# Ten groups of an MLP's up projection by one Strassen step, in a fused encoder layer on one core

## The chip, the cores and the metric

One core of a Trainium2 chip runs the whole layer in one launch. The metric is device microseconds of that launch. Five engines have their own instruction queues and run side by side, held in step by semaphores: TensorE (PE; the loading of its stationary operand is listed apart, as PEld), VectorE (DVE), ScalarE (ACT), GpSimd (POOL) and SyncE (SP), which issues most DMAs.

## The reference

One layer of a streaming encoder on x of 512 tokens by 1024 features, in float32: three mixers and their output projection, cross-attention into 256 memory tokens, and a gated MLP. The change touches the MLP alone, whose weights are 1024 x 5632 (up) and 2816 x 1024 (down); the residual that goes into it is called h2 in the kernel:

```python
def conv_ffn(xn, w_up, conv_w, conv_b, w_down):
    h = xn @ w_up
    a, b = jnp.split(h, 2, axis=-1)
    rhs = conv_w.reshape(CONV_W, 1, D_FF).astype(a.dtype)
    c = lax.conv_general_dilated(a, rhs, window_strides=(1,), padding=[(CONV_W - 1, 0)],
                                 dimension_numbers=('NWC', 'WIO', 'NWC'),
                                 feature_group_count=D_FF) + conv_b
    return (jax.nn.gelu(c, approximate=False) * b) @ w_down
...
        h = h + conv_ffn(rmsnorm(h, ffn_norm_g[l]), ffn_w_up[l], ffn_conv_w[l],
...
```

## The kernel before

All activations lie transposed, features on the 128 partitions and the 512 tokens along the free axis, so a matrix product is a sum over tiles of 128 features. Full float32 accuracy comes from `mm3` (lines 344 to 346): each operand is held as an exact high and low part of 12 bits each, and a product is three matmuls, high by high, high by low, low by high. The parts are made by a copy that rounds (ACT) and a subtraction (DVE): `split` (lines 325 and 326, with a scale 328 and 329) for activations, `_Weights.load` (lines 188 and 191) for weights.

Weights come in the order of their use as units of 128 x 1024, that is four feature tiles by 256 columns, by DMAs on SP (line 186), three units ahead.

The MLP's up projection has 11 groups (`up_group`). A group computes 256 columns of a and the 256 columns of b that are multiplied with them, from four units: a's columns with feature tiles 0 to 3, b's with 0 to 3, a's with 4 to 7, b's with 4 to 7. Each unit is eight products (`funit`), so a group has 4 x 8 x 3 = 96 matmuls with 512 moving columns each. Four PSUM accumulators collect them; tags a0 and a1 hold a, tag b holds b. When they are done, DVE multiplies them by the token's norm factor rb2 (lines 1256 and 1263), ACT starts the convolution (1258), DVE adds the two other taps (1259, 1260), ACT takes the gelu (1261), DVE multiplies (1264), and the result is split at once for the down projection. The norm's gain goes into the split of h2 (line 329, called in `ev_h2`), and rb2 only into the evacuation, so the matmuls of the first group don't wait for the statistics. The down projection reads 22 split tiles; it has 22 units of 24 matmuls and adds the residual.

The order of each engine's instructions is made when the program is built, by a scheduler that simulates the program; the loads of weights are given a high priority. On the chip each engine runs its own list in that order, and an instruction that waits holds up all behind it on its engine.

Of the kernel before, what the change touches and what calls it, by code (L numbers as in the profile page):

```python
# [32 lines left out]
# columns of the packed per-feature vectors  # L33
# [18 lines left out]
def _consts():  # L52
# [19 lines left out]
def _pack(inputs):  # L72
# [43 lines left out]
    wd = f["ffn_w_down"].reshape(NF, P, D).transpose(1, 0, 2)     # [P, NF, D]  # L116
# [43 lines left out]
class _Weights:  # L160
    """Units of the weights in the order of their use: raw, then its two exact parts."""

    def __init__(self, tc, pool, wp, ahead, nraw, nhi, nlo, parts=1):
        self.tc, self.nc, self.pool, self.wp = tc, tc.nc, pool, wp
        self.ahead, self.nraw, self.nhi, self.nlo, self.parts = ahead, nraw, nhi, nlo, parts
        self.n = wp.shape[0]
# [34 lines left out]
    def get(self, width):  # L201
        """The next unit's columns in pieces of this width: a list of (high part, low part)."""
# [8 lines left out]
def trunk_body(ctx: ExitStack, tc: tile.TileContext, A):  # L211
# [3 lines left out]
    sb = ctx.enter_context(tc.tile_pool(name="sb", bufs=1))  # L215
# [51 lines left out]
    # the tensor engine's clock rises before the first operands are there  # L267
    wz = cp.tile([P, 512], mybir.dt.bfloat16, name="wz")
# [5 lines left out]
    # ---------------------------------------------------------------- inputs  # L274
# [9 lines left out]
    def after(ins, earlier):  # L284
        """Issue order of two instructions of one engine."""
# [62 lines left out]
    def funit(pts, acts, ks, first, last):  # L348
        """One [4 k tiles x 256 columns] unit into two accumulators."""
# [20 lines left out]
    def tgroup(acts, nt, evac):  # L370
        """Token layout: [nt x 128 tokens] x 512 columns, in four steps of two k tiles."""
# [17 lines left out]
    def sumsq(tiles, n, alloc, eng=V, behind=()):  # L389
        """Sum over feature tiles of the squares, [P, n]."""  # L390
# [12 lines left out]
    def colsum(tot, n, tag="pr"):  # L403
        """Column form: sums over the partitions, [P tokens, n // P] (in PSUM, stride 2)."""
# [14 lines left out]
    def bcast_cols(r, n, dst):  # L419
        """[P tokens, n // P] -> the same row on every partition, [P, n]."""  # L420
# [8 lines left out]
    # ---------------------------------------------------------------- x  # L429
# [28 lines left out]
    RA = [bs(F32, (P, NC, 128)) for _ in range(2)]     # (r | a)  # L458
# [69 lines left out]
    def tr_rows(dst, q, src):  # L528
        """The rows of two chunks."""
# [8 lines left out]
    # rows (a_j | v_j) of the chunks  # L538
# [37 lines left out]
    # ---------------------------------------------------------------- chunk products  # L576
    # system s = (chunk, head); rows (b_j | k_j), columns (r_t | a_t)
# [36 lines left out]
    for q in range(4):                   # two chunks each  # L614
# [15 lines left out]
    # inverse of (I - T_ab): 32-row blocks by substitution, one system on a partition  # L630
# [45 lines left out]
    # ---------------------------------------------------------------- z_diff  # L676
# [27 lines left out]
    # ---------------------------------------------------------------- diff attention  # L704
# [33 lines left out]
    def diff_s(h, i):  # L738
        """Softmax of a block of queries: the difference of the two, normalized."""
# [564 lines left out]
```

## Time and profile before

| | |
|---|---|
| time, median of 3 runs | 842.74 us (841.8 to 844.15) |
| profiled execution, span | 843.9 us |
| PE busy | 828.0 us, 98% |
| DVE, ACT, POOL busy | 477.0, 376.8, 148.8 us |
| first matmul of group 1 of the up projection | 502.67 us |
| end of the last up group | 720.27 us |

"Busy" is the time in which an engine executes. Ends of matmuls are modelled, so what PE needs is read from the distance of one matmul's start to the next, not from the durations. Line numbers are those of the kernel before; several operations are written by helpers, whose one line then stands for many tiles. A tile's name is that of its tag: wr, wh and wl are the raw, high and low weights.

### The profile page before, as it was taken

How to read it: one execution, taken by the hardware profiler on the slowest of the kernel's cores; microseconds unless marked ns; L12 is line 12 of the kernel's file. 1: busy time of each engine (PE TensorE's matmuls, PEld its weight loads, DVE VectorE, ACT ScalarE, POOL GpSimd, SP SyncE). 2: the span in 40 equal slices, each digit the busy share in tenths (PEclk: the TensorE clock that was granted, in tenths of full speed). 3: DMA queues.
4: the chain of work that ended last, by engine and by line, in shares of the span. 5: the costliest groups of instructions: out<-in, count | busy, mean ns of one | idle time of the engine just before them, and what ended most of it. 6: DMA issues, size and time to landing. Idle time of an engine off the chain costs nothing.

```text
span 843.9 us, 11622 instructions
## 1 busy us (share of the span) xinstructions
PE 828.0 (98%) x4280; PEld 671.2 (80%) x4280; DVE 477.0 (57%) x870; ACT 376.8 (45%) x702; POOL 148.8 (18%) x162
## 2 busy tenths in 40 slices
PE   8998997999999999999999999999999999999998
PEld 5775786878887688888888888888888888888886
DVE  5758389355574683655756655555555556523221
ACT  6343352656464794544655433344333344322220
POOL 5546274482703110001000000000000000000000
PEclk9999998999897999999999999999999999999999
DMA  6422122122121134422111323322232322333321
GB/s 203 150 72 69 36 80 97 39 87 89 51 77 63 47 92 138 136 91 86 63 38 63 108 79 101 100 96 93 100 100 100 99 92 96 102 101 116 121 99 50
DMA packets 42040, 76.34 MB, mean 90 GB/s; under 512 B 4608, under 2 KB 5760, under 8 KB 41984
## 3 DMA queue, kind: packets, MB, share of 16 engines
q1 hardware_dynamic: 39744, 72.46, 25.7%
q10 hardware_dynamic: 2240, 3.15, 1.2%
q8 instruction: 33, 0.54, 0.3%
q14 instruction: 23, 0.19, 0.1%
HBM read 73.50 MB, written 2.10 MB: 90 GB/s over the span
## 4 chain that ended last, share of the span: by engine, by line
PE 85%; DVE 4%; ACT 1%; issue 0%; ACTq 0%; DVEq 0%
PE ps L344 23%; PE ps L345 23%; PE ps L346 23%; DVE b L657 1%; DVE b L656 1%; PE S L344 1%; PE y L931 1%; PE y L928 1%; PE T L587 1%; PE pT L776 1%; PE colsum L407 1%; PE U L824 1%; PE tr L535 1%; PE S L345 1%; PE qkT L730 0%; PE Sx L344 0%
## 5 line engine op out<-in xcount | busy, mean ns | idle before, releaser
L188 ACT ACTIVATE wh<-wr 128x512 fp32r<-128x512 f32 x256 | 160.7, 629 | 274.3 <-PE ps L345 208.8
L191 DVE TENSOR_TENSOR wl<-wr,wh 128x512 fp32r<-128x512 f32 x220 | 153.6, 699 | 166.8 <-ACT wh L188 166.6
L344 PE MATMUL ps<-r,wh 128*128 128x512 f32 x432 | 168.6, 392 | 0.0
L345 PE MATMUL ps<-r,wh 128*128 128x512 f32 x432 | 168.1, 389 | 0.0
L346 PE MATMUL ps<-r,wl 128*128 128x512 f32 x432 | 166.5, 390 | 0.0
L344 PEld LDWEIGHTS ps<-r,wh 128*128 128x128 f32 x432 | 81.1, 188 | 17.3 <-issue 0.5
L345 PEld LDWEIGHTS ps<-r,wh 128*128 128x128 f32 x432 | 81.1, 188 | 17.0 <-issue 0.5
L346 PEld LDWEIGHTS ps<-r,wl 128*128 128x128 f32 x432 | 81.1, 188 | 16.8
L344 PE MATMUL ps<-wh,xh 128*128 128x256 f32 (+1 forms) x224 | 73.8, 352 | 6.8 <-DVE d L329 4.7
L345 PE MATMUL ps<-wl,xh 128*128 128x256 f32 (+1 forms) x224 | 77.8, 347 | 0.2 <-POOL wl L191 0.2
L191 POOL TENSOR_TENSOR wl<-wr,wh 128x512 fp32r<-128x512 f32 x36 | 52.2, 1460 | 33.2 <-ACT wh L188 33.0
L345 PE MATMUL ps<-xl,wh 128*128 128x512 f32 x144 | 57.1, 399 | 0.0
L344 PEld LDWEIGHTS ps<-wh,xh 128*128 128x128 f32 x224 | 43.0, 194 | 14.5 <-DVE d L329 5.0
L345 PEld LDWEIGHTS ps<-wl,xh 128*128 128x128 f32 x224 | 43.6, 195 | 6.2 <-issue 0.7
L344 PE MATMUL ps<-xh,wh 128*128 128x512 f32 x112 | 45.2, 411 | 1.5 <-ACT wh L188 1.4
L346 PE MATMUL ps<-xh,wl 128*128 128x512 f32 x112 | 44.4, 409 | 0.7 <-POOL wl L191 0.6
L345 PE MATMUL ps<-d,wh 128*128 128x512 f32 x112 | 43.9, 392 | 0.0
L346 PE MATMUL ps<-d,wl 128*128 128x512 f32 x112 | 43.7, 390 | 0.0
L344 PE MATMUL ps<-d,wh 128*128 128x512 f32 x112 | 41.6, 391 | 0.0
L346 PE MATMUL ps<-wh,xl 128*128 128x512 f32 x96 | 39.3, 409 | 0.0
L346 PE MATMUL ps<-wh,xh 128*128 128x256 f32 x128 | 37.1, 290 | 0.0
L345 PEld LDWEIGHTS ps<-xl,wh 128*128 128x128 f32 x144 | 27.9, 194 | 6.7 <-issue 0.8
(338 smaller groups left out, 1433.3 us busy)
## 6 DMA issues: line engine op xcount, KB each, us to landing
wr<-in_wp_dram SPq DMA_DIRECT2D x256, 256.0 KB, 2.6
r<-in_xt_dram SPq DMA_DIRECT2D x8, 256.0 KB, 5.5
t<-in_xt_dram ACTq DMA_DIRECT2D x8, 256.0 KB, 3.0
out_dram<-t SPq DMA_DIRECT2D x8, 256.0 KB, 2.4
kv<-in_memt_dram ACTq DMA_DIRECT2D x4, 256.0 KB, 4.2
pm<-in_pmat_dram SPq DMA_DIRECT2D x1, 512.0 KB, 4.2
cs<-in_cst_dram SPq DMA_DIRECT2D x1, 273.0 KB, 3.0
bias<-in_bias_dram SPq DMA_DIRECT2D x1, 256.0 KB, 6.1
```

What stands on the lines that cost most here:

```text
L188: nc.scalar.activation(hi, raw, AF.Copy)
L191: (nc.vector if el == "V" else nc.gpsimd).tensor_tensor(lo, raw, hi.bitcast(F32), ALU.subtract)
L344: mm(out, lh, rh, start=start, stop=False)
L345: mm(out, lh, rl, start=False, stop=False)
L346: mm(out, ll, rh, start=False, stop=stop)
L407: mm(pt[:, 2 * i:2 * i + 2], tot[:, i * P:(i + 1) * P], ones[:, 0:2], start=True, stop=True)
L535: PE.transpose(pv4[0:n, c, p, :], src(p, 2 * q + c), ident)
L587: mm(pts[hh].rearrange("p (c h t) -> p c h t", c=2, h=2)[:, c, p], KB[p][o:o + 64, cg, :], RA[p][o:o + 64, cg, :], start=True, stop=True)
L656: V.tensor_tensor(o, a0, a1, ALU.mult)
L657: V.tensor_tensor(Mi[:, j + 1:32, 0:j], Mi[:, j + 1:32, 0:j], o, ALU.add)
L776: PE.transpose(pt[:, m:m + P], sc0[h, i][:, b * P:(b + 1) * P], ident)
L824: mm(p4[0:64, c, h, :], Y[s // 16][:, s % 16, :], W0[q][:, c, h, :], start=True, stop=True)
```

## The change

Group 0 stays as it is (`_Weights` now ends at unit 66, the end of it), but its results are kept whole instead of split. For the other ten groups (NS is 10) the product is one of 2 x 2 blocks: on one side the unit of weights (feature tiles 0 to 3 or 4 to 7, columns of a or b), on the other side the activations (feature tiles 0 to 3 or 4 to 7, tokens 0 to 255 or 256 to 511). Eight block products become seven by Winograd's form of Strassen's step. Each of the seven is 24 matmuls of 256 moving columns (4 feature tiles, 2 halves of the columns, 3 of `mm3`), so a group has 168 of them.

Added for it: the normalised activations hn, made once (DVE, eight operations); seven blocks of activations, of which four are differences (POOL), each split once; in each group four sums of weight units (POOL) and seven splits of 128 x 1024 (ACT and DVE); evacuations that combine the seven products (ACT and DVE). The norm factor is now in hn and no more in the evacuation. The tiles from the mixers and the attention are released after group 0 (`sbx.close()`), and all later ones lie in a new pool, s2. The 22 splits for the down projection stand behind the up groups in the code. Weight splits are instructions of 1024 columns, not two of 512. The unit order is the same. (In the diff, comments that the change drops are left out.)

```diff
 class _Weights:
...
-        self.n = wp.shape[0]
+        self.n = WFIRST
...
+    sbx = ExitStack()
+    sb = sbx.enter_context(tc.tile_pool(name="sb", bufs=1))
...
-    def up_group(g):
...
+    for c in range(2):
+        a, ca, b = ts(), ts(), ts()
+        V.tensor_tensor(a, pa[c], rb2, ALU.mult)
+        V.tensor_tensor(b, pb[c], rb2, ALU.mult)
+        conv(c, a, ca)
+        ACT.activation(ca, ca, AF.Gelu)
+        mt[c] = dsl()
+        V.tensor_tensor(mt[c], b, ca, ALU.mult)
+    sbx.close()
+    s2 = ctx.enter_context(tc.tile_pool(name="s2", bufs=1, reuse_waits="tile"))
...
+    for k in range(8):
+        V.scalar_tensor_tensor(hn[k // 4][:, k % 4], h2[k], pcol("ffn_norm_g", k), rb2, ALU.mult, ALU.mult)
...
+    def diff(x, y):
+        d = t2("e", 5)
+        G.tensor_tensor(d, x, y, ALU.subtract)
+        return d
+    sx(0, quarter(0, 0))
+    s1 = diff(quarter(1, 0), quarter(1, 1))
+    sx(1, s1)
+    sg = diff(quarter(0, 0), s1)
+    sx(2, sg)
+    sx(3, quarter(0, 1))
+    sx(4, diff(quarter(1, 0), quarter(0, 0)))
+    sx(5, quarter(1, 1))
+    sx(6, diff(quarter(0, 1), sg))
...
+    def wadd(x, y):
+        t = t2("wt", 3)
+        G.tensor_tensor(t, x, y, ALU.add)
+        return t
...
+        if j == 0:
+            wsplit(n, wload(u))
+        elif j == 1:
+            tsum[1] = wadd(raw[u], wload(u + 1))
+            wsplit(n, tsum[1])
+        elif j == 2:
+            tsum[2] = wadd(tsum[1], wload(u + 3))
+            wsplit(n, tsum[2])
+        elif j == 3:
+            wsplit(n, wload(u + 2))
+        elif j == 4:
+            wsplit(n, wadd(raw[u + 1], raw[u + 3]))
+        elif j == 5:
+            wsplit(n, wadd(tsum[2], raw[u + 2]))
+        else:
+            wsplit(n, raw[u + 3])
...
+    def product(n, pt, first):
+        wh, wl = wget(n)
+        sh, sl = SX[n % 7]
+        for c in range(2):
+            for k in range(4):
+                cl = slice(c * P, (c + 1) * P)
+                o = pt[:, c * 256:(c + 1) * 256]
+                for i, (l, r) in enumerate(((wh, sh), (wh, sl), (wl, sh))):
+                    mm(o, l[:, k, cl], r[:, k], start=first and c + k + i == 0,
...
+    for g in range(NS):
+        n = 7 * g
...
+        product(n, x, True)
+        ACT.activation(p1, halves(x), AF.Copy)
+        product(n + 1, y, True)
+        product(n + 2, z, True)
+        V.tensor_tensor(v2, halves(z), p1, ALU.subtract)
+        product(n + 3, x, False)
+        ACT.activation(a[:, :, t0], halves(x), AF.Copy)
+        product(n + 4, z, True)
+        V.tensor_tensor(v3, halves(z), v2, ALU.add)
+        V.tensor_tensor(b[:, :, t1], halves(y), v3, ALU.add)
+        product(n + 5, z, True)
+        V.tensor_tensor(a[:, :, t1], halves(z), v3, ALU.subtract)
+        product(n + 6, y, False)
+        V.tensor_tensor(b[:, :, t0], halves(y), v2, ALU.add)
+        for c in range(2):
+            conv(2 * g + 2 + c, a[:, c], ca[:, c])
+        ACT.activation(ca, ca, AF.Gelu)
...
+            V.tensor_tensor(mt[i], b[:, c], ca[:, c], ALU.mult)
+    for i in range(22):
...
+        split(mt[i], t[:, 0], t[:, 1])
```

Where the instructions stand. On VectorE, at the end of group 0, before (ps_787 and ps_788 are b's two accumulators, wl67 and wl68 low parts of the next units):

```order
L1263 TENSOR_TENSOR t_791_5089<-ps_787_4936,rb_161_881 128x512
L1256 TENSOR_TENSOR t_793_5095<-ps_786_4935,rb_161_881 128x512
L1264 TENSOR_TENSOR t_791_5089<-t_791_5089,t_790_5084 128x512
L191 TENSOR_TENSOR wl67_1_5018<-wr67_1_5016,wh67_1_5017 128x512
L1259 SCALAR_TENSOR_TENSOR t_794_5097<-t_793_5095,pv_75,t_794_5097 128x511
L1263 TENSOR_TENSOR t_795_5102<-ps_788_4937,rb_161_881 128x512
```

and after (ps_788 gets group 0's last matmul; hn are the normalised activations, wlo_824 and sx_800 the low parts of the first product's weights and activations):

```order
L1262 TENSOR_TENSOR t_795_5062<-ps_788_4940,rb_161_884 128x512
L1278 SCALAR_TENSOR_TENSOR hn_797_5075<-d_746_4667,pv_78,rb_161_884 128x512
...
L1278 SCALAR_TENSOR_TENSOR hn_798_5076<-d_771_4893,pv_78,rb_161_884 128x512
L1266 TENSOR_TENSOR d_792_5058<-t_791_5051,t_790_5050 128x512
L1250 SCALAR_TENSOR_TENSOR t_794_5061<-t_793_5060,pv_78,t_794_5061 128x511
L332 TENSOR_TENSOR wlo_824_5129<-wraw_822_5126,whi_823_5128 128x1024
L332 TENSOR_TENSOR sx_800_5086<-hn_797_5075,sx_799_5085 128x1024
```

The eight hn stand behind t_795, which needs group 0's last matmul, and the first product's two low parts stand behind them; before, low parts of the next units lay ahead of and among group 0's evacuations.

On GpSimd, whose list ended with h2_rstd before, the same place after (wt are sums of weight units, e the differences of activations; line 1327 is the weights', 1297 the activations'):

```order
L422 TENSOR_TENSOR h2_rstd_4929<-h2_ms_4922,mhalf_149 128x4
L1327 TENSOR_TENSOR wt_826_5134<-wraw_822_5126,wraw_825_5132 128x1024
L1297 TENSOR_TENSOR e_801_5089<-hn_797_5075,hn_798_5076 128x1024
L1327 TENSOR_TENSOR wt_830_5142<-wt_826_5134,wraw_829_5140 128x1024
L1327 TENSOR_TENSOR wt_837_5180<-wraw_825_5132,wraw_829_5140 128x1024
L1297 TENSOR_TENSOR e_804_5095<-hn_797_5075,e_801_5089 128x1024
L1297 TENSOR_TENSOR e_809_5105<-hn_797_5075 128x1024
L1327 TENSOR_TENSOR wt_841_5211<-wt_830_5142,wraw_833_5148 128x1024
L1297 TENSOR_TENSOR e_814_5115<-hn_798_5076,e_804_5095 128x1024
```

wt_826 can run during group 0; all behind it wait for the last hn, because e_801 does.

On VectorE, a steady group after (wlo are the low parts of weights; 1392, 1398, 1399, 1402 and 1404 are v2, v3, b1, a1 and b0, the evacuations from PSUM):

```order
L1392 TENSOR_TENSOR t_914_5723<-ps_910_5692,t_906_5660 128x512
L332 TENSOR_TENSOR wlo_916_5726<-wraw_892_5581,whi_915_5725 128x1024
L332 TENSOR_TENSOR wlo_920_5758<-wraw_918_5755,whi_919_5757 128x1024
L1398 TENSOR_TENSOR t_921_5785<-ps_917_5754,t_914_5723 128x512
L1399 TENSOR_TENSOR e_899_5626<-ps_902_5629,t_921_5785 128x2x256
L332 TENSOR_TENSOR wlo_926_5794<-wt_924_5791,whi_925_5793 128x1024
L1402 TENSOR_TENSOR e_898_5625<-ps_922_5788,t_921_5785 128x2x256
L332 TENSOR_TENSOR wlo_930_5827<-wt_928_5824,whi_929_5826 128x1024
L1250 SCALAR_TENSOR_TENSOR e_900_5627<-e_898_5625,pv_78,e_900_5627 128x511 x2
L1251 SCALAR_TENSOR_TENSOR e_900_5627<-e_898_5625,pv_78,e_900_5627 128x510 x2
L1404 TENSOR_TENSOR e_899_5626<-ps_902_5629,t_914_5723 128x2x256
L332 TENSOR_TENSOR wlo_940_5874<-wraw_938_5871,whi_939_5873 128x1024
```

Evacuations of one group stand among the low parts of the next; the low parts of wt tiles need POOL's sums.

## Rows read from the trace of the kernel before

**Rows 1.** The page: busy time of PE, granted clock by slice, chain.

```profile
PE 828.0 (98%) x4280; PEld 671.2 (80%) x4280; DVE 477.0 (57%) x870; ACT 376.8 (45%) x702; POOL 148.8 (18%) x162
...
PEclk9999998999897999999999999999999999999999
...
PE 85%; DVE 4%; ACT 1%; issue 0%; ACTq 0%; DVEq 0%
```

**Rows 2.** Timeline of PE, boundaries of groups: start, duration, operation.

```profile
502.67 0.39 PE L344 MATMUL ps<-r,wh 128*128 128x512 f32 x1
...
524.43 0.39 PE L344 MATMUL ps<-r,wh 128*128 128x512 f32 x1
...
720.27 0.39 PE L344 MATMUL ps<-b,wh 128*128 128x512 f32 x1
```

**Rows 3.** Windows: busy time of each engine (instructions), granted clock, DMA share, GB/s.

```profile
309.80:315.50 5.70, 5.70 (x50) 5.70 (x50) 5.21 (x11) 5.56 (x12) 0.00 (x0) 1.00 0.24 60
524.40:546.20 21.80, 21.80 (x98) 18.02 (x97) 13.09 (x22) 8.71 (x15) 0.00 (x0) 1.00 0.31 97
265.40:275.70 10.30, 10.30 (x39) 7.10 (x37) 2.40 (x8) 3.79 (x11) 0.00 (x0) 0.50 0.01 2
...
260.00:265.00 5.00, 5.00 (x41) 3.67 (x40) 0.78 (x1) 0.65 (x3) 1.94 (x3) 1.00 0.32 105
```

**Rows 4.** Timeline of PE: first and last of 48 matmuls of 256 columns.

```profile
309.79 0.33 PE L344 MATMUL ps<-wh,xh 128*128 128x256 f32 x1
...
315.47 0.28 PE L346 MATMUL ps<-wh,xh 128*128 128x256 f32 x1
```

**Rows 5.** Timeline of DVE, end of group 1.

```profile
521.91 0.69 DVE L1263 TENSOR_TENSOR t<-ps,rb 128x512 f32<-128x512 f32 x1 [1.19 <-PE ps L346]
522.52 0.68 DVE L1256 TENSOR_TENSOR t<-ps,rb 128x512 f32<-128x512 f32 x1
523.12 0.68 DVE L1264 TENSOR_TENSOR t<-t,t 128x512 f32<-128x512 f32 x1
523.72 0.69 DVE L191 TENSOR_TENSOR wl<-wr,wh 128x512 fp32r<-128x512 f32 x1
524.42 0.75 DVE L1259 SCALAR_TENSOR_TENSOR t<-t,pv,t 128x511 f32<-128x511 f32 x1
525.09 0.68 DVE L1263 TENSOR_TENSOR t<-ps,rb 128x512 f32<-128x512 f32 x1
```

**Rows 6.** Groups of instructions by form: count, busy us, mean ns, idle before.

```profile
L188 ACT ACTIVATE wh<-wr 128x512 fp32r<-128x512 f32 x256 | 160.7, 629 | 274.3 <-PE ps L345 208.8 <-PE ps L346 23.6 <-DMA wr<-in_wp_dram 20.2
...
L326 DVE TENSOR_TENSOR kv<-pTx,kv 128x256 fp32r<-128x256 f32 x8 | 3.4, 422 | 3.5 <-ACT kv L325 3.5
```

**Rows 7.** Timeline of POOL, operations on two tiles, and one cheaper kind.

```profile
61.43 1.03 POOL L451 TENSOR_TENSOR kv<-kv 128x511 f32<-128x511 f32 x1
...
153.28 1.27 POOL L191 TENSOR_TENSOR wl<-wr,wh 128x512 fp32r<-128x512 f32 x1
...
189.89 0.73 POOL L881 TENSOR_TENSOR mtot<-mtot,t 128x256 f32<-128x256 f32 x1
```

**Rows 8.** Timeline, DVE beside POOL, in two places.

```profile
62.61 2.99 POOL L191 TENSOR_TENSOR wl<-wr,wh 128x512 fp32r<-128x512 f32 x2
...
62.67 1.77 DVE L453 SCALAR_TENSOR_TENSOR r<-kv,pv,kv 128x512 f32<-128x512 f32 x1 [2.53 <-POOL kv L452]
...
64.36 0.68 DVE L449 TENSOR_TENSOR kv<-ps,rb 128x512 f32<-128x512 f32 x1
...
219.09 1.04 POOL L693 TENSOR_TENSOR d<-d,s_r 128x512 f32<-128x512 f32 x1
...
219.44 1.24 DVE L191 TENSOR_TENSOR wl<-wr,wh 128x512 fp32r<-128x512 f32 x1 [2.80 <-ACT wh L188]
```

**Rows 9.** Timeline of PE: two matmuls of 256 columns at the low clock.

```profile
229.73 0.41 PE L346 MATMUL ps<-wh,xh 128*128 128x256 f32 x1
229.94 0.41 PE L344 MATMUL ps<-wh,xh 128*128 128x256 f32 x1
```

More of the change, by code (lines that the diff above doesn't have):

```diff
@@ L221, in slot @@
         cnt[0] += 1
-        return sb.tile(list(shape), dt, name=f"{nm or tag}_{cnt[0]}", tag=tag, bufs=bufs)
+        pool = keep if tag in ("d", "t", "rb") else sb
+        return pool.tile(list(shape), dt, name=f"{nm or tag}_{cnt[0]}", tag=tag, bufs=bufs)
     def xh(dt=F32R, shape=(P, 512)):
@@ L1233, in trunk_body @@
         after(pre_ge, i)
-    def mtile(i):
-        if i < 5:
-            t = bs(F32R, (P, 2, 512))
-        else:
-            f = kvs if i < 9 else pslot if i < 10 else xh if i < 14 else xl if i < 18 else rs if i < 20 else dsl
-            return f(F32R), f(F32R)
-        return t[:, 0], t[:, 1]
-    mt = {}
-    def up_group(g):
-        pa, pb = [ps("a0"), ps("a1")], [ps("b"), ps("b")]
-        funit(pa, h2n, range(0, 4), True, False)
-        funit(pb, h2n, range(0, 4), True, False)
-        funit(pa, h2n, range(4, 8), False, True)
-        funit(pb, h2n, range(4, 8), False, True)
-        cw = lambda tap, i: pv[:, PC["ffn_conv_w"] + 22 * tap + i:PC["ffn_conv_w"] + 22 * tap + i + 1]
-        for c in range(2):
-            i = 2 * g + c
-            a = ts()
-            V.tensor_tensor(a, pa[c], rb2, ALU.mult)
-            ca = ts()
-            ACT.activation(ca, a, AF.Identity, scale=cw(2, i), bias=pcol("ffn_conv_b", i))
-            V.scalar_tensor_tensor(ca[:, 1:S], a[:, 0:S - 1], cw(1, i), ca[:, 1:S], ALU.mult, ALU.add)
-            V.scalar_tensor_tensor(ca[:, 2:S], a[:, 0:S - 2], cw(0, i), ca[:, 2:S], ALU.mult, ALU.add)
-            ACT.activation(ca, ca, AF.Gelu)
-            b = ts()
-            V.tensor_tensor(b, pb[c], rb2, ALU.mult)
-            V.tensor_tensor(b, b, ca, ALU.mult)
-            hi, lo = mtile(i)
-            split(b, hi, lo)
-            mt[i] = (hi, lo)
@@ L1269, in trunk_body, with cw, conv @@
-    for g in range(11):
-        up_group(g)
+    mt = {}
+    def cw(tap, i):
+        return pv[:, PC["ffn_conv_w"] + 22 * tap + i:PC["ffn_conv_w"] + 22 * tap + i + 1]
+    def conv(i, a, ca):
+        ACT.activation(ca, a, AF.Identity, scale=cw(2, i), bias=pcol("ffn_conv_b", i))
+        V.scalar_tensor_tensor(ca[:, 1:S], a[:, 0:S - 1], cw(1, i), ca[:, 1:S], ALU.mult, ALU.add)
+        V.scalar_tensor_tensor(ca[:, 2:S], a[:, 0:S - 2], cw(0, i), ca[:, 2:S], ALU.mult, ALU.add)
+    pa, pb = [ps("a0"), ps("a1")], [ps("b"), ps("b")]
@@ new lines, in trunk_body @@
+    funit(pa, h2n, range(0, 4), True, False)
+    funit(pb, h2n, range(0, 4), True, False)
+    funit(pa, h2n, range(4, 8), False, True)
+    funit(pb, h2n, range(4, 8), False, True)
+    for c in range(2):
[8 more added lines that the diff above has]
+    s2 = ctx.enter_context(tc.tile_pool(name="s2", bufs=1, reuse_waits="tile"))
@@ new lines, in t2, with quarter, sx @@
+    def t2(tag, bufs, shape=(P, 4, 256), dt=F32):
+        cnt[0] += 1
+        return s2.tile(list(shape), dt, name=f"{tag}_{cnt[0]}", tag=tag, bufs=bufs)
+    hn = [t2("hn", 2, (P, 4, 512)) for i in range(2)]
+    for k in range(8):
+        V.scalar_tensor_tensor(hn[k // 4][:, k % 4], h2[k], pcol("ffn_norm_g", k), rb2, ALU.mult, ALU.mult)
+    def quarter(i, j):
+        return hn[j][:, :, i * 256:(i + 1) * 256]
+    SX = {}
+    def sx(j, src):
+        hi, lo = t2("sx", 14, dt=F32R), t2("sx", 14, dt=F32R)
+        split(src, hi, lo)
+        SX[j] = (hi, lo)
@@ new lines, in diff, with wload @@
+    def diff(x, y):
[11 more added lines that the diff above has]
+    sx(6, diff(quarter(0, 1), sg))
+    wp = A["wp"]
+    raw, tsum, WX = {}, {}, {}
+    prep = [0]
+    def wload(u):
+        raw[u] = t2("wraw", 5)
+        nc.sync.dma_start(raw[u].rearrange("p k m -> p (k m)"), wp[u])
+        return raw[u]
@@ new lines, in wsplit, with wprep @@
+    def wsplit(n, src):
+        hi, lo = t2("whi", 4, dt=F32R), t2("wlo", 4, dt=F32R)
+        split(src, hi, lo)
+        WX[n] = (hi, lo)
+    def wadd(x, y):
+        t = t2("wt", 3)
+        G.tensor_tensor(t, x, y, ALU.add)
+        return t
+    NS = 10
+    def wprep(n):
+        if n >= 7 * NS:
+            u = WFIRST + 4 * NS + n - 7 * NS
+            if u < wp.shape[0]:
+                wsplit(n, wload(u))
+            return
+        g, j = divmod(n, 7)
+        u = WFIRST + 4 * g
+        if j == 0:
+            wsplit(n, wload(u))
+        elif j == 1:
[10 more added lines that the diff above has]
+            wsplit(n, wadd(tsum[2], raw[u + 2]))
+        else:
+            wsplit(n, raw[u + 3])
@@ new lines, in wget @@
+    def wget(n):
+        with tc.high_priority():
+            while prep[0] <= n + 3:
+                wprep(prep[0])
+                prep[0] += 1
+        return WX.pop(n)
+    def product(n, pt, first):
+        wh, wl = wget(n)
+        sh, sl = SX[n % 7]
+        for c in range(2):
+            for k in range(4):
[3 more added lines that the diff above has]
+                    mm(o, l[:, k, cl], r[:, k], start=first and c + k + i == 0,
+                       stop=c == 1 and k == 3 and i == 2, skip_group_check=not first)
@@ new lines, in halves @@
+    def halves(pt):
+        return pt.rearrange("p (c t) -> p c t", c=2)
+    t0, t1 = slice(0, 256), slice(256, 512)
+    for g in range(NS):
+        n = 7 * g
+        a, b, ca = (t2("e", 5, (P, 2, 512)) for _ in range(3))
+        x, y = ps("b"), ps("pr")
+        product(n, x, True)
+        p1 = ts(F32, (P, 2, 256))
+        ACT.activation(p1, halves(x), AF.Copy)
+        product(n + 1, y, True)
+        z = ps("a0")
+        product(n + 2, z, True)
+        v2 = ts(F32, (P, 2, 256))
+        V.tensor_tensor(v2, halves(z), p1, ALU.subtract)
+        product(n + 3, x, False)
+        ACT.activation(a[:, :, t0], halves(x), AF.Copy)
+        z = ps("a1")
+        product(n + 4, z, True)
+        v3 = ts(F32, (P, 2, 256))
+        V.tensor_tensor(v3, halves(z), v2, ALU.add)
+        V.tensor_tensor(b[:, :, t1], halves(y), v3, ALU.add)
+        z = ps("pd")
+        product(n + 5, z, True)
[6 more added lines that the diff above has]
+        for c in range(2):
+            i = 2 * g + 2 + c
+            if 8 <= i < 16:
+                if i % 4 == 0:
+                    mq = t2("hn", 2, (P, 4, 512))
+                mt[i] = mq[:, i % 4]
+            else:
+                mt[i] = dsl() if i < 8 else t2("mt", 6, (P, 512))
+            V.tensor_tensor(mt[i], b[:, c], ca[:, c], ALU.mult)
@@ L1271, in trunk_body, with dunit @@
+    mx = {}
+    for i in range(22):
+        tag, bufs = ("sx", 14) if i < 14 else ("wt", 3) if i < 17 else ("e", 5)
+        t = t2(tag, bufs, (P, 2, 512), F32R)
+        split(mt[i], t[:, 0], t[:, 1])
+        mx[i] = (t[:, 0], t[:, 1])
+    nd = [7 * NS]
+    def dunit():
+        nd[0] += 1
+        h, l = wget(nd[0] - 1)
+        return [(h[:, j], l[:, j]) for j in range(4)]
     for gp in range(2):
@@ L1274, in trunk_body @@
             for g in range(2):
-                funit(pts[2 * g:2 * g + 2], mt, range(4 * q, 4 * q + 4), q == 0, False)
-        w = W.get(256)
+                w = dunit()
+                for j in range(4):
+                    for c in range(2):
+                        sl = slice(c * P, (c + 1) * P)
+                        mm3(pts[2 * g + c], w[j][0][:, sl], w[j][1][:, sl], *mx[4 * q + j],
+                            q == 0 and j == 0, False)
+        w = dunit()
         for g in range(2):
```

9 lines of the change are left out of this document (5 added, 4 removed).

## The prediction

> **What bounds the kernel now.** I read the page's engine shares and chain first: PE is busy for 98% of the span and carries 85% of the chain, at a granted clock in the top tenth almost throughout [rows 1]. The end moves only with PE's work, or with something that makes PE wait. Then the boundaries of the MLP's groups on PE: group 0 gives way to group 1 at 502.67 us, the next boundary is 524.43, and the last up group ends at 720.27 [rows 2]. A group takes 21.76 us, which is 96 matmuls at 0.2267, and the ten groups that the change touches take 217.6. Then the window of one group: PE 21.80 of 21.80, DVE 13.09, ACT 8.71, POOL nothing, clock 1.00 [rows 3]. DVE stands idle for 40% and waits for PE where it does [rows 5]; POOL is free. The question is what PE gains and whether DVE and POOL can still feed it.
>
> **PE's own work.** Ten groups go from 96 matmuls of 512 columns to 168 of 256. A run of 256-column products lies in the attention: 48 of them from 309.79 to 315.47 [rows 4], 0.1209 each with a slower first one, 0.12 in the steady rows. 168 x 0.1195 = 20.1 us; the gain is at most 1.68 us a group, 16.8 in all. Everything else is weighed against that.
>
> **DVE's work per group.** Its operations are pitched closer than their durations: a 128x512 tensor_tensor follows another after 0.60 to 0.61 us, a scalar_tensor_tensor takes 0.67 of the queue [rows 5]. A 128x256 one lasts 0.42 against 0.69 [rows 6], so 256 columns more cost 0.27, and a 128x1024 one, which this trace does not hold, is pitched 0.60 + 2 x 0.27 = 1.14. In the changed order a group has seven low parts at 1.14 (8.0), five evacuations at 0.60 (3.0), four taps at 0.67 (2.7) and two products at 0.60 (1.2): 14.9 us, still under PE's 20.1. ACT has two copies, two identities and a gelu beside seven high parts; with 0.63 per 512 columns [rows 6], and twice that as the upper end for 1024, that is under 14 us, hidden. Weight bytes are the same, on the same queue; DMA is busy a third of the time in a group [rows 3].
>
> **The adds on POOL, and what they do to DVE.** Each group adds four 128x1024 tensor_tensor on POOL. Adds of two tiles take 0.73 us at 256 columns and 1.27 at 512 [rows 7], so 0.54 per 256 columns and 2.35 for 1024 (lower end 2.06, twice the 1.03 of the cheaper row; upper end 2.54). Alone that is 9.4 of 20, hidden. But POOL and DVE do not run side by side on SBUF data: at 62.61 two POOL operations take 2.99 together, and the DVE operation that began 0.06 us later took 1.77 where its kind takes 0.75; at 219.44 a low part beside a 1.04 us POOL operation took 1.24 for 0.69. A DVE operation that reads PSUM passes: 0.68 at 64.36, inside the POOL pair [rows 5, 8]. So POOL's 512 columns hold DVE back 1.02 + 0.06 = 1.08 us, and 1024 hold 1.08 + 1.08 = 2.16 (ends: 1.9 from the cheaper kind, 2.35 for the whole operation). The low parts, the taps and the mults all read two SBUF tiles. In the order after, the adds follow low parts, and only v2 and a1 (PSUM) stand where an add can run beside them: 1.2 us saved. A steady group then takes DVE 14.9 + 4 x 2.16 - 1.2 = 22.3 us, more than PE's 20.1 and more than the 21.76 of before. DVE becomes the bound, and PE waits on low parts. Ends: 20.1 (the adds fit wholly into DVE's waits, PE binds) to 23.6 (no operation passes).
>
> The Trainium skill (SBUF — State Buffer, section Who interferes with whom) says that of a GpSimd operation and a DVE operation that share the port pair, the second to start blocks fully until the first ends. The trace shows 1.08 of 1.27 [rows 8], a little less than the whole; by the rule the hold is 2.35, a group 23.1, and the end would be 886 instead of 877.
>
> **The transition.** The new activation blocks need hn, and on DVE the eight hn operations stand behind t_795, which waits for the last matmul of group 0 (502.67). Nothing of the seven products can begin before, so PE runs dry there: the old order had group 1's weights and operands ready. From 502.67 DVE has 0.3 of wait, t_795 0.6, eight hn 5.4, a product 0.6, a tap 0.67, the first weight's low part 1.14 and the first block's 1.14: 9.8 us; with three POOL adds between them (behind hn, e_801, wt_830 and wt_837 can run back to back) 16.3. PE then goes product by product as low parts arrive. Up to the low part of the next group's first product, DVE has 15 operations of 1.14, four of 0.60, eight hn and two taps at 0.67 and the wait: 17.1 + 2.4 + 5.4 + 1.3 + 0.3 = 26.5; POOL has ten adds in that stretch (wt_830 to wt_872 and four differences): 21.6; one evacuation passes. 26.5 + 21.6 - 0.6 = 47.5 us (ends: 30 with no hold, when PE binds after the first 9.8, and 50).
>
> **The end of the up projection.** From the last group's first low part DVE has 6 low parts, 4 taps, 7 small ones, and six of the 22 splits of the MLP's activations, which now come here instead of group by group: 6.8 + 2.7 + 4.2 + 3.6 + four adds 8.6 - 1.2 = 24.7; five more such splits and two more low parts 5.9 before PE's row may go on; then 14 matmuls of 0.2267 and a product of 24 x 0.1195 (6.0), less the 47 matmuls of the down projection that the order has already run there (10.7): 26.0. The splits before cost nothing on PE, and nothing is gained by them.
>
> **Sum.** 47.5 + 8 x 22.3 + 26.0 = 251.9 against 217.6: +34.3 us. The profiled span of 843.9 lies 1.15 over the median of the runs, 842.74; 843.9 + 34.3 = 878.2, and at the median's level **877 us**.
>
> **What can go otherwise.** *A, faster:* POOL's adds cost DVE nothing, because they fall into its waits or the hold is not exclusive at this size. Then the transition costs the 9.8 us before the first product, and one product at the low clock after the gap: the granted clock was 0.50 (1.2 GHz) in 265.4 to 275.7, behind a stretch of small matmuls at 1.00, and 256-column matmuls were pitched 0.213 at that level [rows 3, 9]; 24 x (0.213 - 0.12) = 2.2. The groups bring -16.8: 9.8 + 2.2 - 16.8 = -4.8, 838 us. For it: DVE's 14.9 leaves 5 us a group. Against it: an add holds 2.16 and four do not fit in 5 us. It decides from a hold under (20.1 - 14.9 + 1.2) / 4 = 1.6 us an add, and in the transition, where DVE has no waits, only from none at all.
> *B, the hold costs in the transition alone:* 47.5, eight groups at PE's 20.1, the last 23: 231.3, +13.7, 856 us. 14.9 + 8.6 less all five evacuations (3.0) is 20.5: it needs every one of them to pass beside an add, where the order puts two there.
> *C, cheaper adds* (hold 1.9): 26.5 + 19.0 - 0.6 = 44.9, groups 21.3, last 25.0: 240.3, +22.7, 865 us; it lies within the forecast's own range.
> *D, the low clock lasts:* if PE's waits for DVE keep the clock at 0.50, a group takes 168 x 0.213 = 35.8, and ten of them +140, near 980 us. The rows show the low level only around small and waiting matmuls, and 1.00 in every window of long products; PE would wait 2 us of 22 here.
> *E, loads of weights bind:* 168 loads of 0.19 each would be 32 us a group, +100, 943 us. The 48 products of 256 columns, with PEld busy 5.70 of 5.70, were pitched 0.12 all the same [rows 3, 4], so loads overlap one another.
> The Trainium skill (Perfetto Trace Analysis, section Identifying the Most-Contended Engine) wants TensorE's headroom judged by the busy share of the weight loads, 18.02 of 21.80 in a group [rows 3]; by that rule twice the loads per column would leave none, and E's 943 would be the time. The trace does not agree in the only place where it shows this.
>
> **Chances.** Forecast with C inside, 72%: 860 to 892, its own range. B 12% (850 to 862). A 11%, from 834 to 848. D 4%, E 1%. What a measurement of this kernel can tell from no change is about 0.3%, 840.2 to 845.3. Faster takes most of A, 8%; same the rest of it, 3%; slower 89%. Range 851 to 893: it takes in B, C and the upper ends of hold and transition, and leaves A and D out.
>
> **What would show it.** In the profile after: PE idle of 10 to 16 us right behind 502, ended by DVE's sx low part; the first boundary of a Strassen group (first product to first product) about 38 to 48 us on, then steady ones near 22.3, with PE busy near 20.1 of that, and PE's waits released by DVE wlo at line 332; mean durations of wlo well above 1.23 us (0.69 + 2 x 0.27), of POOL's adds above 2.35. The chain passes from PE to DVE there. Steady groups of 20.1 with PE full would make the hold the wrong step; a first product before 510 would make the transition wrong; 24 matmuls taking over 2.9 us without a wait would make the PE term wrong.

## The result and the profile after

The changed kernel takes 881.97 us (median of 4 runs, 879.12 to 889.16) against 843.44 of before: 1.046 times as long, 95% interval [1.041, 1.051]. The forecast was 877, inside 851 to 893, and slower. The profiled execution has a span of 879.5 us.

The page of the changed kernel, the lines that answer to [rows 1] (busy time, granted clock by slice, the chain by engine), and two groups of instructions, the low parts of the weights on DVE and the weight sums on POOL (count | busy us, mean ns | idle before):

```profile
PE 823.4 (94%) x5000; PEld 699.0 (79%) x5000; DVE 602.7 (69%) x863; ACT 407.5 (46%) x687; POOL 277.4 (32%) x206
...
PEclk9999999999976999999999959999999999999999
...
PE 65%; DVE 25%; issue 5%; ACT 3%; POOL 2%; DMA 0%; SPq 0%; ACTq 0%; DVEq 0%; POOLq 0%
...
L332 DVE TENSOR_TENSOR wlo<-wraw,whi 128x1024 fp32r<-128x1024 f32 x52 | 93.5, 1809 | 58.5 <-ACT whi L331 58.5
...
L1327 POOL TENSOR_TENSOR wt<-wt,wraw 128x1024 f32<-128x1024 f32 x20 | 56.6, 2828 | 83.8 <-issue 83.8
```

PE has fallen from 98% to 94%, and a quarter of the chain is DVE's, which had 4%. Group 0's last matmul starts at 500.94, so it is over at 501.16. DVE behind that point:

```profile
501.89 0.68 DVE L1262 TENSOR_TENSOR t<-ps,rb 128x512 f32<-128x512 f32 x1
502.49 5.38 DVE L1278 SCALAR_TENSOR_TENSOR hn<-d,pv,rb 128x512 f32<-128x512 f32 x8
507.79 0.68 DVE L1266 TENSOR_TENSOR d<-t,t 128x512 f32<-128x512 f32 x1
508.39 2.82 DVE L1250 SCALAR_TENSOR_TENSOR t<-t,pv,t 128x511 f32<-128x511 f32 x1
511.14 3.36 DVE L332 TENSOR_TENSOR wlo<-wraw,whi 128x1024 fp32r<-128x1024 f32 x1
514.43 3.35 DVE L332 TENSOR_TENSOR sx<-hn,sx 128x1024 fp32r<-128x1024 f32 x1
```

POOL in the same stretch:

```profile
498.24 2.40 POOL L1327 TENSOR_TENSOR wt<-wraw,wraw 128x1024 f32<-128x1024 f32 x1 [9.97 <-DMA wraw<-in_wp_dram]
507.95 2.72 POOL L1297 TENSOR_TENSOR e<-hn,hn 128x1024 f32<-128x1024 f32 x1 [7.31 <-DVE hn L1278]
510.63 2.78 POOL L1327 TENSOR_TENSOR wt<-wt,wraw 128x1024 f32<-128x1024 f32 x1
513.38 3.32 POOL L1327 TENSOR_TENSOR wt<-wraw,wraw 128x1024 f32<-128x1024 f32 x1
```

and PE, whose idle time and its releaser stand in brackets (the last two rows are the low part of the first product of the second Strassen group, and of the tenth):

```profile
506.43 0.58 PE L1374 MATMUL ps<-sx,whi 128*128 128x256 f32 x1 [5.10 <-ACT sx L331]
517.84 0.58 PE L1374 MATMUL ps<-sx,whi 128*128 128x256 f32 x1 [10.83 <-DVE sx L332]
...
549.76 0.38 PE L1374 MATMUL ps<-sx,wlo 128*128 128x256 f32 x1 [1.89 <-DVE wlo L332]
...
732.02 0.38 PE L1374 MATMUL ps<-sx,wlo 128*128 128x256 f32 x1 [0.20 <-DVE wlo L332]
```

The eight hn follow t_795 at once; from then on DVE and POOL take turns: the tap lasts 2.82 instead of 0.75, the low parts 3.36 and 3.35 instead of 1.21. PE does one matmul at 506.43 and then waits 10.83 for the low part sx. Windows of the transition and of a steady group (they answer to [rows 3]):

```profile
643.99:666.75 22.76, 20.92 (x171) 20.31 (x170) 22.73 (x19) 10.52 (x12) 11.80 (x5) 1.00 0.28 92
506.40:549.70 43.30, 23.06 (x146) 22.16 (x146) 43.30 (x24) 16.44 (x18) 30.77 (x10) 0.75 0.14 49
```

DVE is busy for 22.73 of 22.76. In the transition it is busy throughout, with PE at 23 of 43 us. Between 549.76 and 732.02 lie eight groups, 22.78 us each, where [rows 2] have 21.76.

### The profile page after: what moved, and what is told of

Read it like the earlier page. It is cut to its first block, busy times and chain, and to the rows that moved or that the text cites. A ratio compares the mean times of both kernels' runs of the same rounds, so it can differ in the third digit from the quotient of the medians.

```text
span 879.5 us, 12893 instructions
## 1 busy us (share of the span) xinstructions
PE 823.4 (94%) x5000; PEld 699.0 (79%) x5000; DVE 602.7 (69%) x863; ACT 407.5 (46%) x687; POOL 277.4 (32%) x206
## 4 chain that ended last, share of the span: by engine, by line
PE 65%; DVE 25%; issue 5%; ACT 3%; POOL 2%; DMA 0%; SPq 0%; ACTq 0%; DVEq 0%; POOLq 0%
PE ps L350 15%; PE ps L351 15%; PE ps L352 15%; DVE wlo L332 11%; PE ps L1374 4%; DVE e L1250 3%; DVE sx L332 1%; DVE b L663 1%; DVE b L662 1%; PE S L350 1%; PE y L934 1%; PE y L937 1%; PE T L593 1%; DVE e L1251 1%; POOL wl L193 1%
## 5 line engine op out<-in xcount | busy, mean ns | idle before, releaser
L1374 PE MATMUL ps<-sx,whi 128*128 128x256 f32 x1120 | 210.2, 288 | 36.5 <-DVE sx L332 18.4
L1374 PEld LDWEIGHTS ps<-sx,whi 128*128 128x128 f32 x1120 | 178.7, 195 | 41.0 <-DVE sx L332 19.1
L1374 PE MATMUL ps<-sx,wlo 128*128 128x256 f32 x560 | 160.7, 288 | 4.1 <-DVE wlo L332 4.1
L190 ACT ACTIVATE wh<-wr 128x512 fp32r<-128x512 f32 x132 | 82.7, 629 | 114.4 <-PE ps L351 44.0
L332 DVE TENSOR_TENSOR wlo<-wraw,whi 128x1024 fp32r<-128x1024 f32 x52 | 93.5, 1809 | 58.5 <-ACT whi L331 58.5
L1374 PEld LDWEIGHTS ps<-sx,wlo 128*128 128x128 f32 x560 | 109.3, 195 | 6.0 <-DVE wlo L332 6.0
L193 DVE TENSOR_TENSOR wl<-wr,wh 128x512 fp32r<-128x512 f32 x96 | 68.3, 712 | 48.8 <-ACT wh L190 48.6
L1327 POOL TENSOR_TENSOR wt<-wraw,wraw 128x1024 f32<-128x1024 f32 x20 | 60.8, 3038 | 28.9 <-DVE wlo L332 19.0
L332 DVE TENSOR_TENSOR wlo<-wt,whi 128x1024 fp32r<-128x1024 f32 x40 | 68.9, 1736 | 0.4 <-ACT whi L331 0.4
L351 PE MATMUL ps<-sx,whi 128*128 128x512 f32 x112 | 43.6, 389 | 0.0
L350 PE MATMUL ps<-sx,whi 128*128 128x512 f32 x112 | 43.6, 389 | 0.0
L352 PE MATMUL ps<-sx,wlo 128*128 128x512 f32 x112 | 43.2, 390 | 0.3 <-DVE wlo L332 0.3
```

The lines of the kernel that those rows point to most:

```text
L190: nc.scalar.activation(hi, raw, AF.Copy)
L193: (nc.vector if el == "V" else nc.gpsimd).tensor_tensor(lo, raw, hi.bitcast(F32), ALU.subtract)
L332: V.tensor_tensor(dlo, src, dhi.bitcast(F32), ALU.subtract)
L350: mm(out, lh, rh, start=start, stop=False)
L351: mm(out, lh, rl, start=False, stop=False)
L352: mm(out, ll, rh, start=False, stop=stop)
```

## The experiments

In all of them, T is the end of group 0's last matmul, and "T to second group" the time from there until PE starts its 169th matmul of the ten groups, so that one group's number of 168 is behind it (51.3 us in the changed kernel; PE's order mixes neighbouring products, so this matmul need not be one of the second group). T itself lies between 500 and 507 us from one run to the next, and 200 us ahead of T the runs are already nearly as far apart; times counted from T leave that out.

**The sums left out.**

```diff
     def wadd(x, y):
-        t = t2("wt", 3)
-        G.tensor_tensor(t, x, y, ALU.add)
-        return t
+        return y
```

> The four weight sums of each group are left out: the second term's unit is split in their place, so the output is not the layer's; the four differences of activations stay on POOL. Theory (POOL's adds hold VectorE back about 2.2 us each, and that makes VectorE the bound): VectorE's 14.9 us a group fit under PE's 20.2, so a steady group falls from 22.8 to 20.2 to 20.8, the low part of the next group's first product comes 35 us behind group 0's end instead of 48.5, and the profiled span falls by about 33 us to 846 (840 to 853). Rival 1 (PE waits 1.7 us a group for ACT's copy of product 0, which stands behind a gelu that waits for the taps; the loop over PE, ACT and VectorE sets the pace and the sums matter only by their latency): a steady group stays above 22, span 865 to 870. Rival 2 (256-column matmuls are slower in place than in the attention's run): groups stay near 22.8 with PE busy all the time.

Measured: 850.93 us, 1.006 times before [1.002, 1.010]; span 849.1. Eight steady groups of 20.16 each, T to second group 43.2. The low part of the second group's first product comes 40.5 behind T, not 35: in that run DVE waits for ACT's high parts from 533 on, and PE has no gap from 524.4. One steady group, in the window view:

```profile
604.49:624.65 20.16, 20.16 (x170) 20.16 (x169) 15.51 (x19) 10.66 (x12) 0.00 (x0) 1.00 0.30 105
```

PE is full, with 168 matmuls at 0.12, and DVE is at 15.51. Rival 1 falls: the loop over ACT's copy and the gelu is still there and costs nothing. Rival 2 falls as well. The loss of a steady group is the four sums.

**Sums and differences on VectorE.**

```diff
-        G.tensor_tensor(t, x, y, ALU.add)
+        V.tensor_tensor(t, x, y, ALU.add)
...
-        G.tensor_tensor(d, x, y, ALU.subtract)
+        V.tensor_tensor(d, x, y, ALU.subtract)
```

> All sums and differences move from POOL to VectorE, nothing is left out. Theory (hold): an add costs VectorE 1.14 of its own instead of the 2.2 of a hold, so a group is 14.9 + 4.6 = 19.5 us of VectorE, under PE's 20.2; steady group 20.2 to 20.8, transition 26.5 + 10 x 1.14 = 38 instead of 48.5, span about 850 (843 to 857). Rival (no hold; the 1024-column operations are slow in themselves, 1.75 us on average as the profile's group of rows says): VectorE has 4 x 1.75 more to do, a group takes 27 or more, span above 915.

Measured: 856.17 us, 1.013 [1.010, 1.016]; span 853.7; groups of 21.02, T to second group 41.8, the low part of the second group's first product 39.6 behind T, where 38 was expected. A steady group in the window view:

```profile
604.81:625.83 21.02, 20.42 (x171) 20.21 (x170) 19.55 (x23) 10.64 (x12) 0.00 (x0) 1.00 0.29 101
```

DVE's 19.55 is what was expected; the group lies 0.2 above its range (the fifth buffer, below, bears on that). The busiest engine of the feeding side was given four more operations a group, and the kernel became 26 us shorter. The rival said 915. What an add costs DVE as its own work (1.14) is about half of what it costs there as POOL's.

**hn earlier.** hn is computed ahead of group 0's evacuations, in memory of the pool that stays:

```diff
+    hn = [hnt() for i in range(2)]
+    for k in range(8):
+        V.scalar_tensor_tensor(hn[k // 4][:, k % 4], h2[k], pcol("ffn_norm_g", k), rb2, ALU.mult, ALU.mult)
     for c in range(2):
         a, ca, b = ts(), ts(), ts()
         V.tensor_tensor(a, pa[c], rb2, ALU.mult)
...
-    hn = [t2("hn", 2, (P, 4, 512)) for i in range(2)]
...
```

> hn is made before group 0's evacuations, in memory that is kept, so it no longer stands behind t_795 and group 0's last matmul; POOL's sums and differences stay. (The warm-up at the start has 16 matmuls of 256 columns instead of 8 of 512, for room.) Theory: the transition loses hn's 5.4 us and the differences that POOL can now make while VectorE waits, 6 to 12 us in all; steady groups stay at 22.8; span 868 to 874. Rival (the transition's cost is VectorE's and POOL's total work, and moving hn only displaces group 0's evacuations): gain under 3 us, span 877 or more.

Measured: 880.42 us, 1.041 [1.038, 1.045]; span 877.8, 1.7 under the changed kernel; T to second group 47.9 instead of 51.3, steady groups 22.79. T comes 2.1 later in this run, so from T to the last matmul's end it gains 3.8 us (370.6 for 374.4): far less than the theory's 6 to 12 and a little more than the rival's 3. The rival is the nearer one. ACT's row for the norm factor, and DVE's for hn, show why it could gain little:

```profile
496.62 0.60 ACT L433 ACTIVATE rb<-bc 128x512 f32<-128x512 f32 x1 [8.17 <-PE bc L432]
```

```profile
497.25 5.39 DVE L1265 SCALAR_TENSOR_TENSOR hn<-d,pv,rb 128x512 f32<-128x512 f32 x8 [6.19 <-ACT rb L433]
```

The factor that hn multiplies by comes from a matmul placed in the second half of group 0, T is at 503.2, and hn ends only 0.7 us before it. DVE and POOL then have the same sums and low parts left, and four of group 0's evacuations, which now stand behind hn (502.56 to 504.95 on DVE), take part of what was won.

**Blocks early.** Both edits above, and the seven blocks of activations stand ahead of group 0's evacuations in the code:

```diff
     sx(6, diff(quarter(0, 1), sg))
+    for c in range(2):
+        a, ca, b = ts(), ts(), ts()
+        V.tensor_tensor(a, pa[c], rb2, ALU.mult)
...
```

> Sums and differences on VectorE, hn before group 0's evacuations, and the seven blocks ahead of group 0's evacuations in the code. Theory: transition about 30 us (38 less hn's 5.4 and some of the blocks that are made while PE still runs group 0), steady groups 20.2 to 20.8, span about 842 (835 to 850), so about as fast as the kernel before, since PE's gain of 1.6 us a group in ten groups about pays for what the transition still costs. Rival (no hold): slower than 900.

Measured: 854.66 us, 1.011 [1.009, 1.014]; span 852.4; T to second group 39.1, not 30; groups of 21.02. The theory's size was off: DVE is busy from 495.27, when hn begins, without a gap to the second group. PE's row in a steady group names its one wait there:

```profile
621.97 0.39 PE L1379 MATMUL ps<-sx,whi 128*128 128x256 f32 x1 [0.60 <-ACT whi L331]
```

From matmul to matmul that place takes 0.88, and the next one 0.22, where the others take 0.12. The run with sums and differences on VectorE alone has the same 0.88 in one place of a group.

**A fifth buffer for high parts.** The same kernel with

```diff
-        hi, lo = t2("whi", 4, dt=F32R), t2("wlo", 4, dt=F32R)
+        hi, lo = t2("whi", 5, dt=F32R), t2("wlo", 4, dt=F32R)
```

> The run with sums and differences on VectorE, hn and blocks early, and of the three later edits only the fifth buffer for high parts of weights (and, for room, a small constant moved to the pool that is released). If PE's 0.88 us wait a group was for such a buffer: steady groups 20.16 instead of 21.02, the stretch from group 0's end to the second Strassen group unchanged at 38 to 40, span about 845. If the wait was for VectorE's total of 19.5 us a group: groups stay at 21.0 and the fifth buffer did nothing in the later kernel either.

Measured, one run: 848.23 us beside 845.97 of before; span 846.4; groups of 20.16, T to second group 38.9. A steady group in the window view:

```profile
603.00:623.16 20.16, 20.16 (x170) 20.16 (x169) 19.48 (x23) 10.77 (x13) 0.00 (x0) 1.00 0.32 106
```

The wait was for a buffer: DVE at 19.48 of 20.16 is no bound.

**The transition taken apart.** On top of that, the order around group 0's end: the matmuls of its second half (first_mm) come behind the broadcast of the norm factor (bc_ins), the weights of the first four products (PRE is 3) are prepared before the blocks, hn (i) comes behind the second product's low part (LAST is 1), and group 0's evacuations come behind hn:

```diff
+    for m in first_mm:
+        after(m, bc_ins[-2])
...
+    with tc.high_priority():
+        while prep[0] <= PRE:
+            wprep(prep[0])
+            prep[0] += 1
...
+        after(i, WL[LAST])
```

> On top of the run with sums and differences on VectorE and hn and blocks early, three more edits: the broadcast matmul of the norm factor goes ahead of the second half of group 0's matmuls (it came at 493.6 there, its input was ready at 489); the first two products' weights and their sums are prepared ahead of hn, while VectorE waits for that factor; and the high parts of weights have five buffers, not four. Theory (what is left of the cost is VectorE's work between group 0's end and the next group, and a wait of 0.9 us a group for a buffer of high parts): end of group 0 to first matmul of the second Strassen group about 29 us instead of 39, steady groups 20.2 instead of 21.0, span about 16 us less than 852, near 836 (832 to 843), so 0.3 to 1 percent faster than before. Rival (the low clock and first waits of PE behind group 0's end set the transition, not VectorE's work): the stretch stays above 35 us, span 845 or more.

Measured: 842.91 us (12 runs, 837.43 to 846.72) against 844.59 (17 runs); ratio 0.997 [0.995, 0.999]. T to second group is 30.9, groups 20.16, and from T to the last matmul's end 332.0 us; it is 337.5 in the kernel before and 374.4 in the changed one. So this version is faster than both, by 0.3% over before. The profiled span, 842.8, lies in its range but above the 836, with T at 506.8 in that run; the order of every engine up to group 0's second half is that of the kernel before this edit, and the run is 4 us behind that kernel's already 200 us ahead of T, so the lateness is not the edit's, and why the earlier part scatters by some microseconds stays open. Nearly all of the transition in the window view:

```profile
507.00:537.70 30.70, 24.63 (x169) 24.07 (x169) 30.70 (x32) 15.65 (x19) 0.00 (x0) 0.83 0.16 54
```

By its own mark of 35 us the rival falls. DVE has no gap from T to the second group in either run, with 41 operations before this edit and 33 now: the stretch went with VectorE's work. What the earlier broadcast and the earlier weights each brought was not taken apart. About 10 us of loss are left in it, 30.9 less 20.2.

**Copies for sums.** The changed kernel with a one-tile operation on POOL:

```diff
-        G.tensor_tensor(t, x, y, ALU.add)
+        G.tensor_copy(t, y)
```

> The changed kernel, with each weight sum on POOL replaced by a copy of its second term on POOL (so the output is not the layer's). POOL reads one tile instead of two. If a hold on VectorE's two-tile operations comes with every POOL operation on SBUF for about its length: low parts that fall beside a copy are still stretched, by the copy's length, and a steady group is about 14.9 + 4 copies less 1.2, so between 20.2 and 22.8, as the copy is cheaper than an add. If the hold needs two tiles read on both sides: low parts all take 1.2 us, steady group 20.2, span about 846 to 850.

Measured, one run: 856.31 us, span 854.5; groups of 20.16. In the transition, a block's low part on DVE, and the copy on POOL that it met:

```profile
533.52 2.06 DVE L332 TENSOR_TENSOR sx<-hn,sx 128x1024 fp32r<-128x1024 f32 x1
```

```profile
532.53 1.97 POOL L1327 COPY wt<-wraw 128x1024 f32<-128x1024 f32 x1 [2.05 <-DVE wlo L332]
```

A copy alone takes 1.04. Here it took 0.93 longer and held the low part back by 0.85 (2.06 less 1.21). A POOL operation that reads one tile holds too, at most for about its length. In a steady group little of that is left. Two taps, and the copy that they met:

```profile
609.38 2.19 DVE L1250 SCALAR_TENSOR_TENSOR e<-e,pv,e 128x511 f32<-128x511 f32 x2
```

```profile
609.53 1.50 POOL L1327 COPY wt<-wraw 128x1024 f32<-128x1024 f32 x1 [1.54 <-DVE wlo L332]
```

They take 2.19 for 1.40, one low part takes 1.37 for 1.21, and the other copies meet a wait of DVE or an operation from PSUM; DVE's busy time is 16.37 a group, where the run without sums has 15.51. So the copies show the hold, but not what four full holds of that length would do. The two ends named beforehand differ in how long such operations last, not in the group's time, which is PE's 20.16 for both.

**Sums in the kernel before.**

```diff
+    dm = kvs()
+    for k in range(88):
+        G.tensor_tensor(dm, h2[k % 8], h2[(k + 1) % 8], ALU.add)
     for g in range(11):
         up_group(g)
```

> The kernel before, with 88 sums of 128x512 on POOL ahead of the up projection, into a tile that nobody reads. If POOL's adds hold VectorE back by 1.08 us each: while they run, 18 of VectorE's 22 operations in a group wait, 13.1 + 18 x 1.08 = 32 us a group instead of 21.76, for the about five groups that 88 adds last; span longer by 30 to 65 us. If the hold is an effect of 1024-column operations or of the Strassen order: no change, 843.

Measured, one run: 882.11 us beside 844.59, span 880.3. While the sums run (494 to 641 us), from one group's first evacuation of b to the next it is 28.6 us; behind them it is 21.76 again. DVE in that stretch, with 512 columns an operation (tap, evacuation from PSUM, low part, product):

```profile
510.70 1.77 DVE L1259 SCALAR_TENSOR_TENSOR t<-t,pv,t 128x511 f32<-128x511 f32 x1
512.40 0.68 DVE L1263 TENSOR_TENSOR t<-ps,rb 128x512 f32<-128x512 f32 x1
...
515.80 1.78 DVE L191 TENSOR_TENSOR wl<-wr,wh 128x512 fp32r<-128x512 f32 x1
517.50 1.77 DVE L1264 TENSOR_TENSOR t<-t,t 128x512 f32<-128x512 f32 x1
```

Most operations on two SBUF tiles take 1.7 to 1.8 for 0.69 to 0.75, and all 20 that read PSUM in that stretch 0.67 to 0.69. Sums that nobody reads, on an engine that had been idle, cost 37.5 us. 28.6 is below the 32 that was worked out: some pass more cheaply, one of a group's two products at 0.67 (it follows two evacuations from PSUM), the splits at 0.98 to 1.18, and four of ten first taps (line 1259) at 1.52.

## Why the prediction was right, step by step

| step | forecast, us | measured, us |
|---|---|---|
| PE's own group, 168 matmuls | 20.1 | 20.16, where nothing makes it wait |
| pitch of a 1024-column low part | 1.14 | 1.13 to 1.14 from row to row where POOL is idle; each lasts 1.21 |
| hold of one add of 1024 columns | 2.16 | 2.15 (3.36 less 1.21) in the transition; less in a steady group, see below |
| T to the first product's low part | 16.3 | 16.7 (517.84) |
| T to the next group's first low part | 47.5 | 48.6 (549.76) |
| a steady group | 22.3 | 22.78 |
| last group's first low part to the down projection's share | 26.0 | 23.7 |
| the ten groups in all | 251.9 | 254.6 |

The 23.7 are 875.60 (end of the last matmul) less 732.02, less the 119.87 that the down projection takes by itself in the kernel before (840.14 less 720.27). 254.6 less 217.6 is 37.0, and the profiled span grew by 35.6, because T came 1.5 earlier; the medians differ by 38.5.

*The transition* is 1.1 longer than its sum. DVE's rows hold the ten stretched operations of the sum; t_795 starts 0.7 behind T instead of 0.3, and the one evacuation that was to pass (v2, at 542.27) meets no add, which is the other 0.6.

*The steady group* was mis-sized by 0.5 us. 14.9 of own work and four holds of 2.15 are 23.5; 22.78 leaves 0.7 for operations that pass, where the prediction took 1.2 for v2 and a1. DVE's and POOL's rows of one group show it (x2 are two in a row):

```profile
656.83 0.68 DVE L1392 TENSOR_TENSOR t<-ps,t 128x512 f32<-128x512 f32 x1
657.43 6.17 DVE L332 TENSOR_TENSOR wlo<-wraw,whi 128x1024 fp32r<-128x1024 f32 x2
...
665.97 0.68 DVE L1402 TENSOR_TENSOR e<-ps,t 128x512 f32<-128x512 f32 x1
666.57 3.11 DVE L332 TENSOR_TENSOR wlo<-wt,whi 128x1024 fp32r<-128x1024 f32 x1
669.61 3.55 DVE L1250 SCALAR_TENSOR_TENSOR e<-e,pv,e 128x511 f32<-128x511 f32 x2
```

```profile
655.90 3.27 POOL L1327 TENSOR_TENSOR wt<-wt,wraw 128x1024 f32<-128x1024 f32 x1 [6.08 <-issue]
659.13 3.38 POOL L1327 TENSOR_TENSOR wt<-wraw,wraw 128x1024 f32<-128x1024 f32 x1
666.19 2.41 POOL L1327 TENSOR_TENSOR wt<-wt,wraw 128x1024 f32<-128x1024 f32 x1 [3.67 <-issue]
669.82 2.79 POOL L1327 TENSOR_TENSOR wt<-wraw,wraw 128x1024 f32<-128x1024 f32 x1 [1.22 <-DVE wlo L332]
```

v2 (656.83) lies wholly beside an add, a1 (665.97) only with its second half, since the add starts at 666.19. From row to row the holds are 3.8 on the two low parts at 657.43, 1.9 on the one at 666.57 and 2.15 on the taps at 669.61: 7.9, and with 14.9 the 22.8. Eight groups make 4 us of the difference, more than the whole miss of 2.7.

*The end of the up projection* was 2.3 too dear, and here the path was wrong, so that it came out as near as this is luck. The prediction adds up VectorE's work, with four adds. POOL's last add starts at 734.56, and it is the only one behind 732.02. What is left there for PE is 190 matmuls of the ten groups, 22.8 us at 0.12, and PE's waits in that stretch make up the other 0.9: PE sets the end, not VectorE. (By the prediction's own prices its five splits and two low parts are 5.3, not 5.9.)

*The chain.* The forecast said that PE's waits would be released by wlo. In a steady group it is also ACT's copy of the first product, and behind it DVE. The chain of waits through half a group (start, length, what):

```profile
654.33 3.15 PE ps L1374 x24
657.48 0.03 DVEq L332
657.51 1.00 DVE wlo L332
658.51 1.67 issue
660.18 3.42 DVE wlo L332
663.60 0.61 DVE t L1398
```

PE's longest wait of a group is put down to that copy:

```profile
654.33 0.50 PE L1374 MATMUL ps<-sx,whi 128*128 128x256 f32 x2 [1.54 <-ACT t L1387]
```

On ACT the copy stands behind a gelu that waits for DVE's taps. The 1.67 that the chain calls "issue" is DVE between two low parts that show 6.17 us for two, that is, both held by POOL's adds. In the run without sums the copy stands behind the gelu on ACT as well, and PE has no such wait, so the copy is where the wait surfaces, not its cause.

*What stood behind t_795.* The prediction put hn behind group 0's last matmul. That is so in the order, and the rows agree (hn starts 0.6 after t_795 does), but the run with hn earlier shows it to be the smaller reason: the norm factor is there only at 495 to 497, and the work from there on is what fills the 48 us.

*The rivals.* A needed a hold under 1.6 us an add: with the copies, which hold for 0.85 at most, the groups do run at 20.16, which agrees with that point, and the adds lie above it (7.9 for four). B is refuted by the steady groups of 22.78. D: the clock did fall, in the transition alone, and it was back at 1.00 from 538.3 on, though PE still waited in every group. E: the weight loads fill 20.16 of 20.16 us in the run without sums, and the matmuls keep their 0.12. The Trainium skill's hold for the whole instruction (SBUF — State Buffer, section Who interferes with whom) is again a little more than the rows show: 2.15 of an add that takes 2.40 alone. By the rows the sum is 877, by the rule 886; 882 lies between, which does not decide for either: of the 5 us above the sum the trace accounts for 2.7 (4 from operations that do not pass and 1 from the transition, less 2.3 at the end), and the rest is no more than the scatter of the runs, 879.12 to 889.16.

## What to carry to other kernels

An idle engine is not free help: before work is moved to it, look in the trace for the two engines' operations side by side, and count what the moved work holds the busy engine back as work of that engine; here 1.14 us on the busy engine beat up to 2.15 us of hold from the idle one. Dropping an eighth of PE's columns gains only if every engine that feeds it fits into the shorter group, so make the sum for the new length and not for the old one. Where a loop's operands are made anew, the first turn pays their whole preparation; placing part of it into the stretch before, together with the small broadcast that its inputs wait for, took 8 of 38.9 us off the transition here.

## What the runs showed of the hardware

A copy on POOL (one tile read) held a VectorE operation on two SBUF tiles back by 0.85 us where the copy alone takes 1.04; an add that takes 2.40 alone held one back by 2.15. VectorE's operations from PSUM were not held, 0.68 us beside back-to-back adds in the changed kernel and in the kernel before with sums added. In the changed kernel PE's granted clock was 0.50, the low level (1.2 GHz), from 504.2 to 521.3, beginning within the first of PE's two long waits behind group 0 (5.1 and 10.8 us), and again for 3.4 us from 524.7 and from 534.9, beginning in or just behind two later waits of 2.6 and 5.0 us; it rose each time while PE was at work. In the 43 us of the transition the mean is 0.75, with 40 of 146 matmuls pitched 0.213 and most others 0.12; in steady groups, where PE waits some 2 us of 22.8, it stayed at 1.00.
